# The last MLP of a transformer block: two feature groups by pairs of tiles, and a second product by blocks with seven products of sums

## The chip, the cores and the metric

One core of one Trainium2 chip runs the whole kernel. Its engines work side by side, each through its own queue of instructions: TensorE (PE, products; PEld is its weight load), VectorE (DVE), ScalarE (ACT), GpSimd (POOL) and SyncE (SP, which here only issues transfers). The metric is device microseconds (us) of one launch. An execution taken by the profiler gives the trace; its span is the time from its first to its last instruction.

## The reference, cut to what matters

One block on 1024 tokens of width 1024 in float32: a mixer of two attention kinds, an attention over 256 memory rows, and an MLP with 4096 features, each added to its input. What the change touches is the MLP:

```python
def _sq_relu_mlp(h, w_ff_in, w_ff_out):
    return jnp.square(jax.nn.relu(h @ w_ff_in)) @ w_ff_out
...
        x = x + _sq_relu_mlp(_rms_norm(x, norm3_g[l]), w_ff_in[l], w_ff_out[l])
```

`w_ff_in` is 1024x4096 and `w_ff_out` 4096x1024, both float32.

## The kernel before

**Tiles and split products.** Tokens are handled in 8 tiles of 128 rows. A float32 product is made of three products of a reduced type (float32r): every operand is split into a high part (`hi`, a rounded copy) and a low part (`lo`, the rest), and hi·hi, hi·lo and lo·hi are added in PSUM (`mm`, L218). `split_w` (L244 and L249) does this for weights: ACT copies `hi`, and the subtraction for `lo` is done by POOL or by DVE as the list `PLAN_TAIL` says; in the last part it is ("ag", "av", "ag"), so two of three subtractions are POOL's. A few products (W_out, W_xq, W_xo in the stage `between`) use whole float32 operands instead, one instruction that shows as two records in the trace.

**Order of the work.** A scheduler writes out the order in which each engine's instructions stand, from a model of their lengths; on the chip each engine then takes its queue strictly in that order, and waits where an operand or a buffer is not ready. Buffers are rings (`RINGS`): a tag has a number of buffers, and a new tile waits until the tile that many places before it is done with. The PSUM tags of the main part are S, PT and D with 2 buffers each, and PV and M with 1.

**Stages.** `attend` runs the attention of all tiles; beside it `fill` runs the rest: `between` (output projection, memory attention, L902 on) for tiles 0-1 and 2-3, `mlp` for tiles 0-3, and `between` for tiles 4-5. Behind the attention, `between` for tiles 6-7 is merged with what is left of `fill`. Last comes `mlp(d2, 4, 4, x2s)`, the MLP of tiles 4 to 7, with nothing beside it. Tiles 4 and 5 have been stored to DRAM by then (`x2_dr`) and are read back; tiles 6 and 7 are kept on chip.

**The MLP.** It normalises and transposes the four tiles (`norm_T2`: ACT square L293, POOL power L231, DVE scaling L297, PE transposes L274, copies L235 and L236), then takes the 4096 features in 8 groups of four times 128 (`f4`). In each group: 96 products of 512 columns make the features of all four tiles (4 features x 8 slices of the width x 3); for each feature ACT does relu and square (L1034, L1035) and POOL the split (L1037, L1038). Then 96 products of 512 columns multiply them by a slice of `w_ff_out` (2 column halves x 4 tiles x 4 features x 3), and DVE adds each of the 8 PSUM results to the tile (`add_to`, L899). The weights come in 256 KB loads issued by SP (L254). In the last group each finished half tile is stored (L1057).

Of the kernel before, what the change touches and what calls it, by code (L numbers as in the profile page):

```python
# [9 lines left out]
F32 = mybir.dt.float32  # L10
F32R = mybir.dt.float32r
# [5 lines left out]
AF = mybir.ActivationFunctionType  # L17
ALU = mybir.AluOpType
# [4 lines left out]
P = 128  # L23
L = 1024
DM = 1024
# [7 lines left out]
NCMP = 63  # L33
KG = 2
NS = 4
RINGS = {
    "p1": {"x4": 5, "st": 2, "relu": 4, "wraw": 4, "whi": 6, "wlo": 6, "c8": 4, "c4": 2, "kraw": 5, "pc": 2},
    "p2": {"x4": 3, "st": 1, "relu": 2, "whi": 4, "wlo": 4, "c8": 3, "c4": 1, "kraw": 4, "pc": 2},
    "dn": {"b4": 4, "h": 8, "relu": 2, "wraw": 2, "whi": 4, "wlo": 4},
    "d2": {"b4": 4, "h": 8, "relu": 2, "wraw": 3, "whi": 6, "wlo": 6},  # L40
}
PSUMS = {"p1": {"D": 4, "M": 3, "C": 1}, "main": {"S": 2, "PT": 2, "PV": 1, "D": 2, "M": 1}}
TAGS = {"p1": ("D", "M", "C"), "p2": ("D", "M", "D"), "dn": ("D", "M"), "d2": ("S", "PT")}
PLAN_HEAD = ("ag", "av")
PLAN_MAIN = ("ag",)
PLAN_TAIL = ("ag", "av", "ag")

SLC, WIN, DSA, IDX = 0, 2, 4, 5

# [31 lines left out]
REST = 70.0  # L81


def drain(gen):
    for _ in gen:
        pass
# [19 lines left out]
def merge(a, b):  # L106
    drain(beside(*a, *b))
# [59 lines left out]
def build(nc, tc, I, C, out):  # L167
    v, s, g, te = nc.vector, nc.scalar, nc.gpsimd, nc.tensor
    ctx = ExitStack()
    W = {n: I[n][0] for n in I}  # L170
# [7 lines left out]
    p1 = p1_pool.__enter__()  # L178
    psum.update(pool=p1_psum.__enter__(), n=PSUMS["p1"])

    def pst(tag, shape):
        return psum["pool"].tile(shape, F32, tag=tag, name="ps" + tag, bufs=psum["n"][tag],
                                 padded_shape=[P, 512 // int(np.prod(shape[2:]))] + list(shape[2:]))

    def ring(pool, tag, shape, dt=F32):
        n = RINGS[pool.name if isinstance(pool.name, str) else "dn"][tag]
        return pool.tile(shape, dt, tag=tag, name=tag, bufs=n)

    def row(ap):
        return ap[None, :]  # L190
# [26 lines left out]
    def mm(o, a, b, start, stop):  # L217
        te.matmul(o, a, b, start=start, stop=stop)  # L218
# [21 lines left out]
    def split_w(raw, hi, lo):  # L240
        h, l = plan["w"][plan["i"] % len(plan["w"])]
        plan["i"] += 1
        if h == "a":
            s.activation(hi, raw, AF.Copy)  # L244
        elif h == "v":
            v.tensor_copy(hi, raw)
        else:
            g.tensor_scalar(hi, raw, 1.0, 1.0, op0=ALU.mult, op1=ALU.mult)
        (v if l == "v" else g).tensor_tensor(lo, raw, hi, op=ALU.subtract)  # L249
# [40 lines left out]
    def norm_T2(pool, x_t, gb, xs):  # L290

        ss = small(pool, "nss", 1)
        s.activation(xs[0], x_t.rearrange("p (k c) -> p k c", c=P), AF.Square, accum_out=ss)  # L293
        r = rsqrt_of(pool, ss, DM, 1, "n")
        for c in range(0, DM, 512):
            xn = ring(pool, "relu", [P, 512])
            v.scalar_tensor_tensor(xn, x_t[:, c:c + 512], r[:, 0:1], gb[c // 512], op0=ALU.mult, op1=ALU.mult)  # L297
            to_T(pool, xn, [x[:, c // P:c // P + 4] for x in xs], 4)
# [65 lines left out]
    x2_dr = [dr.tile([P, DM], F32, tag=f"x2{t}", name=f"x2{t}") for t in range(NT)]  # L364
# [534 lines left out]
            v.tensor_tensor(dst, pt, dst, op=ALU.add)  # L899
        return add_to  # L900

    def between(pool, t0, nt, x2s, keep):  # L902

        o_of = []
        for t in range(nt):
# [1 line left out]
            for c in range(8):  # L907
                nc.sync.dma_start(o[:, c, :], oT_dr[t0 + t][c])
            o_of.append(o)
        x2 = [ring(pool, "b4", [P, DM]) for t in range(nt)]  # L910
        for t in range(nt):
            nc.sync.dma_start(x2[t], I["x"][0, (t0 + t) * P:(t0 + t + 1) * P, :])
        add_to = residual_add(x2)
# [2 lines left out]
        _, xf, xt_of = xT(pool, nt, True)  # L916
# [85 lines left out]
    def mlp(pool, t0, nt, x2s):  # L1002
# [13 lines left out]
        for f4 in range(8):  # L1016
# [24 lines left out]
            for c in range(2):  # L1041
# [4 lines left out]
                for t in range(nt):  # L1046
# [11 lines left out]
                                          x2[t][:, c * 512:(c + 1) * 512])  # L1058
                    yield 2.6

    def pe_stack():
        pe = p1.tile([P, 2, 32], F32R, tag="pe", name="pe")
        pe2 = ring(p1, "relu", [P, 2, 2, 64])
        for j in range(2):
            nc.sync.dma_start(pe2[0:32, :, j, :], W["nsa_cmp_pe"].rearrange("k l d -> l k d"))
        pp = pst("M", [P, 2, 32])
        for kv in range(2):
            te.transpose(pp[:, kv, :], pe2[0:32, kv, :, :].rearrange("p a d -> p (a d)"), ident[0:32, 0:32])
        s.activation(pe, pp, AF.Copy)
        v.tensor_tensor(pe[64:128], pp[64:128], pe[64:128], op=ALU.subtract)  # L1070
        return pe
# [45 lines left out]
    rest = fill()  # L1117
    together(attend(aw, st), rest, projected)
    aw_pool.__exit__(None, None, None)
    at_pool.__exit__(None, None, None)  # L1120
    d2_pool = tc.tile_pool(name="d2", bufs=1, side="right", reuse_waits="tile")
    plan["w"] = PLAN_TAIL
    d2 = d2_pool.__enter__()
    x2s = {}
    rest = (w for w in rest if not isinstance(w, tuple))
    merge((rest, REST), (between(d2, 6, 2, x2s, True), 45.0))
    dn_pool.__exit__(None, None, None)
    drain(mlp(d2, 4, 4, x2s))
    d2_pool.__exit__(None, None, None)
    ctx.close()  # L1130


# [19 lines left out]
```

## Time and profile before

| | |
|---|---|
| median of 3 runs | 1837.35 us (1835.46 to 1839.35) |
| time of the profiled execution | 1835.75 us |
| its span, first to last instruction | 1833.9 us |
| mean granted TensorE clock | 0.970 of full speed |
| PE busy, share of the span | 1726.9 us, 94% |
| DVE, ACT, POOL busy | 936.1, 1074.6, 895.0 us |
| last MLP, first product to last | from 1468.8 to 1830.2 us |

Times in the trace are us from the start of the span. Busy time of a matmul includes its passage through the array, which overlaps the next one; the rate of products is read from the distance of their starts. A bracket behind a row names the idle time ahead of the instruction and what ended it. Some matmul records are missing from a trace, so starts are counted over whole patterns (hi·hi, lo·hi, hi·lo repeat in threes).

### The profile page before, as it was taken

The page shows a single profiled execution, that of the slowest core. Times are in us where ns is not written, and L with a number is a line of the kernel's source. Part 1 is how long each engine was busy: PE and PEld are TensorE (multiplying, and loading weights), DVE is VectorE, ACT ScalarE, POOL GpSimd, SP SyncE. Part 2 cuts the span into 40 slices and gives each one's busy share as a digit, 9 for nine tenths or more (in the row PEclk, how much of TensorE's full clock was granted, in tenths as well). Part 3 has the DMA queues.
Part 4 walks back from the last instruction along what each step waited for, and adds up shares of the span by engine and source line. Part 5 has one row for each costly group of instructions (what it writes and reads, how often), then busy time and mean ns, then how long its engine had stood idle before and what let it go on. Part 6 is the DMA issues. An engine that isn't in the chain of part 4 may idle for free. (4 is left out here: it accounts for less than half of the span.)

```text
span 1833.9 us, 28049 instructions
## 1 busy us (share of the span) xinstructions
PE 1726.9 (94%) x9262; PEld 1474.2 (80%) x9262; DVE 936.1 (51%) x2353; ACT 1074.6 (59%) x2687; POOL 895.0 (49%) x1034
## 2 busy tenths in 40 slices
PE   5996999889989998999999999999999799999999
PEld 5995988777878787778887788888988578787787
DVE  4553766575684678466664656646523422222222
ACT  4444658889588669955797457994412323333332
POOL 2364657446262244677676576662111144454443
PEclk9997998999999999999999999999989799999999
DMA  8224512256335320222112112125394222222232
GB/s 203 70 87 160 103 34 79 78 193 180 122 112 162 120 81 24 73 81 71 64 63 91 54 65 75 60 79 185 99 288 131 71 69 92 92 93 93 94 99 98
DMA packets 180081, 187.50 MB, mean 102 GB/s; under 512 B 34656, under 2 KB 149088, under 8 KB 179936
## 3 DMA queue, kind: packets, MB, share of 16 engines
q1 hardware_dynamic: 172000, 175.23, 30.8%
q0 software_dynamic: 7936, 10.49, 2.2%
q8 instruction: 73, 1.20, 0.3%
q14 instruction: 72, 0.59, 0.1%
HBM read 164.69 MB, written 20.97 MB: 101 GB/s over the span
## 5 line engine op out<-in xcount | busy, mean ns | idle before, releaser
L249 POOL TENSOR_TENSOR wlo<-wraw,whi 128x512 fp32r<-128x512 f32 (+1 forms) x230 | 308.5, 1347 | 278.7 <-ACT whi L244 247.6
L244 ACT ACTIVATE whi<-wraw 128x512 fp32r<-128x512 f32 (+2 forms) x289 | 181.1, 628 | 247.4 <-PE psS L218 147.1
L218 PE MATMUL psD<-whi,xh 128*128 128x256 f32 (+1 forms) x704 | 193.8, 359 | 3.6 <-ACT whi L244 2.9
L218 PE MATMUL psD<-wlo,xh 128*128 128x256 f32 (+1 forms) x704 | 194.8, 357 | 0.8 <-DMA wlo<-in_w_in_dram 0.8
L236 DVE TENSOR_TENSOR pl<-psPT,ph 128x512 fp32r<-128x512 f32 (+1 forms) x232 | 142.2, 621 | 78.2 <-ACT ph L235 75.4
L218 PE MATMUL psD<-whi,h 128*128 128x512 f32 x512 | 174.3, 404 | 1.8 <-POOL h L1037 1.0
L688 ACT ACTIVATE S<-S,mn 128x128 f32<-128x128 f32 (+7 forms) x192 | 142.7, 744 | 41.5 <-DVE mn L686 40.3
L218 PE MATMUL psS<-whi,h 128*128 128x512 f32 x512 | 162.1, 392 | 5.1 <-DVE b L899 5.1
L693 POOL TENSOR_SCALAR S<-S,sums,gi 128x640 f32<-128x640 f32 (+7 forms) x128 | 107.7, 850 | 106.7 <-DVE sums L691 99.0
L235 ACT ACTIVATE ph<-psPT 128x512 fp32r<-128x512 f32 (+1 forms) x232 | 122.8, 540 | 60.9 <-PE psPT L703 54.5
L249 DVE TENSOR_TENSOR wlo<-wraw,whi 128x512 fp32r<-128x512 f32 (+1 forms) x59 | 64.3, 1090 | 166.9 <-ACT whi L244 166.8
L218 PEld LDWEIGHTS psD<-whi,xh 128*128 128x128 f32 x704 | 134.0, 198 | 14.3 <-ACT whi L244 3.3
L218 PEld LDWEIGHTS psD<-wlo,xh 128*128 128x128 f32 x704 | 134.8, 197 | 12.5 <-DMA wlo<-in_w_in_dram 1.2
L703 PE MATMUL psPT<-c_ident,S 128*128 128x128 f32 x816 | 132.3, 279 | 8.3 <-DVE ql L236 4.2
L899 DVE TENSOR_TENSOR b<-psS,b 128x512 f32<-128x512 f32 (+1 forms) x80 | 50.0, 635 | 152.6 <-PE psS L218 152.6
L218 PEld LDWEIGHTS psS<-whi,h 128*128 128x128 f32 x512 | 96.1, 188 | 29.3 <-DVE b L899 9.3
L218 PE MATMUL psS<-K,qh 128*128 128x384 f32 (+3 forms) x288 | 113.5, 397 | 5.6 <-DVE mn L686 2.8
L218 PEld LDWEIGHTS psD<-whi,h 128*128 128x128 f32 x512 | 95.6, 190 | 23.7 <-DVE b L899 1.5
L703 PEld LDWEIGHTS psPT<-c_ident,S 128*128 128x128 f32 x816 | 98.1, 143 | 18.9 <-POOL S L693 5.6
L218 PE MATMUL psD<-wlo,h 128*128 128x512 f32 x256 | 102.5, 404 | 1.3 <-POOL wlo L249 1.3
L218 PE MATMUL psD<-xh,wlo 128*128 128x512 f32 x256 | 101.5, 398 | 0.0
L899 DVE TENSOR_TENSOR b<-psD,b 128x512 f32<-128x512 f32 (+1 forms) x112 | 63.2, 572 | 74.5 <-PE psD L218 73.0
(299 smaller groups left out, 4647.4 us busy)
## 6 DMA issues: line engine op xcount, KB each, us to landing
wraw<-in_w_ff_in_dram SPq DMA_DIRECT2D x128, 256.0 KB, 2.7
wraw<-in_w_ff_out_dram SPq DMA_DIRECT2D x128, 256.0 KB, 2.6
whi<-in_w_out_dram SPq DMA_DIRECT2D x32, 256.0 KB, 5.0
wlo<-in_w_out_dram SPq DMA_DIRECT2D x32, 256.0 KB, 4.6
wraw<-in_w_in_dram SPq DMA_DIRECT2D x24, 256.0 KB, 3.1
q<-st SPq DMA_DIRECT2D x12, 512.0 KB, 2.6
qin<-q SPq DMA_DIRECT2D x44, 128.0 KB, 2.3
x<-in_x_dram SPq DMA_DIRECT2D x8, 512.0 KB, 5.2
```

Of the source, the lines that this page charges most:

```text
L218: te.matmul(o, a, b, start=start, stop=stop)
L235: s.activation(hi, src, AF.Copy)
L236: v.tensor_tensor(lo, src, hi, op=ALU.subtract)
L244: s.activation(hi, raw, AF.Copy)
L249: (v if l == "v" else g).tensor_tensor(lo, raw, hi, op=ALU.subtract)
L688: s.activation(S, S, AF.Exp, bias=low, scale=-1.0, accum_out=sums[:, hh:hh + 1])
L693: g.tensor_scalar(Ss[hh], Ss[hh], sums[:, hh:hh + 1], 1.0 if gate is None else gate[:, hh:hh + 1], op0=ALU.mult, op1=ALU.mult)
L703: te.transpose(p2[:, j, hh, :], S[:, (c + j) * P:(c + j + 1) * P], ident)
L899: v.tensor_tensor(dst, pt, dst, op=ALU.add)
```

## The change

`mlp` for tiles 4-7 is replaced by `mlp_tail`. Feature groups 0 and 1 (`G = 2`) are done for tiles 4-5 first (`group(f4, (0, 1), False)`) and for tiles 6-7 at the very end (`group(f4, (2, 3), ...)`), each time with 256 columns in the first product, and with their weights loaded and split once for each pair. The other six groups are done for all four tiles between the two (`group_seven`). Their first product is as before. Their second product is cut into 2x2 blocks, on the side of the features (two halves of the tokens by two halves of the group's features) and on the side of `w_ff_out` (two halves of the features by two halves of the columns), and seven block products of sums and differences take the place of eight (Strassen's method in Winograd's form). Each of the seven is 2 tiles x 2 features x 3 = 12 products of 512 columns, so 84 in place of 96. The sums of features (`rows`, 512 columns) and of weights (`cols`, 1024 columns) are DVE's, four of each for a group; each operand is split after its sum is taken, so there are 14 weight splits in place of 8 and 7 feature splits in place of 4. The seven results are summed over the six groups in `acc` (14 additions for a group; copies by ACT in the first), and `put_together` adds them to the tiles at the end: 7 DVE additions of 1024 columns and 8 of 512.

`PLAN_TAIL` is now ("ag", "av"): every second weight subtraction is DVE's. Weight loads of this part are 512 KB each. Rings of the stages concerned get other sizes, and the pool of the new part (`d3`) lies where the pool of `fill` (`dn`) lay. The order in which the engines' instructions stand is the same as before up to the last part of `between` for tiles 4-7.

```diff
+G = 2
 RINGS = {
...
-    "d2": {"b4": 4, "h": 8, "relu": 2, "wraw": 3, "whi": 6, "wlo": 6},
+    "res": {"b4": 4},
+    "d2": {"b4": 2, "h": 8, "relu": 2, "whi": 4, "wlo": 4},
+    "d3": {"g": 2, "h": 12, "relu": 2, "wraw": 4, "whi": 10, "wlo": 10},
+    "d4": {"r": 2, "hsum": 4, "wsum": 3},
...
-PLAN_TAIL = ("ag", "av", "ag")
+PLAN_TAIL = ("ag", "av")
...
+        def features(f4, ts):
+            cols = slice(ts[0] * P, (ts[-1] + 1) * P)
+            for f2 in range(2):
+                gr = []
+                for k0 in range(0, 8, 4):
+                    c0 = (f4 * 4 + f2 * 2) * P
+                    raw = ring(pool, "wraw", [P, 4, 256])
+                    nc.sync.dma_start(raw, W["w_ff_in"][k0 * P:(k0 + 4) * P, c0:c0 + 256].rearrange("(k p) n -> p k n", p=P))
+                    for k in range(0, 4, 2):
+                        hi, lo = ring(pool, "whi", [P, 2, 256], F32R), ring(pool, "wlo", [P, 2, 256], F32R)
+                        split_w(raw[:, k:k + 2, :], hi, lo)
...
+        def down(pt, hs, ws, us):
+            for f, ((hh, hl), (wh, wl)) in enumerate(zip(hs, ws)):
+                mm(pt, hh[:, us], wh, f == 0, False)
+                mm(pt, hh[:, us], wl, False, False)
+                mm(pt, hl[:, us], wh, False, f == len(hs) - 1)
...
+            def product(i, a, b):
+                hh, hl = ring(pool, "h", [P, 2, 256], F32R), ring(pool, "h", [P, 2, 256], F32R)
+                s.activation(hh, a, AF.Copy)
+                g.tensor_tensor(hl, a, hh, op=ALU.subtract)
+                ws = []
+                for f in range(2):
+                    hi, lo = ring(pool, "whi", [P, 512], F32R), ring(pool, "wlo", [P, 512], F32R)
+                    split_w(b[:, f, :], hi, lo)
+                    ws.append((hi, lo))
+                for t in range(2):
+                    pt = pst(("D", "S", "PT")[(2 * i + t) % 3], [P, 512])
+                    down(pt, [(hh[:, f, :], hl[:, f, :]) for f in range(2)], ws, slice(t * P, (t + 1) * P))
+                    if f4 == G:
+                        s.activation(acc[:, i, t, :], pt, AF.Copy)
+                    else:
+                        v.tensor_tensor(acc[:, i, t, :], pt, acc[:, i, t, :], op=ALU.add)
+
+            product(0, A[0][0], B[0][0])
+            product(1, A[0][1], B[1][0])
+            s1 = rows(A[1][0], A[1][1], ALU.add)
+            t1 = cols(B[0][1], B[0][0])
+            product(4, s1, t1)
+            s2, t2 = rows(s1, A[0][0]), cols(B[1][1], t1)
+            product(5, s2, t2)
+            product(3, A[1][1], cols(t2, B[1][0]))
+            product(2, rows(A[0][1], s2), B[1][1])
+            product(6, rows(A[0][0], A[1][0]), cols(B[1][1], B[0][1]))
...
+        for ts in ((0, 1), (2, 3)):
+            for t in ts:
+                start(t)
+            if ts[0] == 0:
+                for f4 in range(G):
+                    group(f4, ts, False)
+        with tc.tile_pool(name="d4", bufs=1, side="right", reuse_waits="tile") as more:
+            acc = more.tile([P, 7, 2, 512], F32, tag="acc", name="acc")
+            for f4 in range(G, 8):
+                group_seven(more, f4, acc)
+            put_together(acc)
+        for t in (0, 1):
+            nc.sync.dma_start(out[0, (t0 + t) * P:(t0 + t + 1) * P, :], x2[t])
+        for f4 in range(G):
+            group(f4, (2, 3), f4 == G - 1)
...
-    drain(mlp(d2, 4, 4, x2s))
     d2_pool.__exit__(None, None, None)
+    with tc.tile_pool(name="d3", bufs=1, reuse_waits="tile") as d3:
+        mlp_tail(d3, res, x2s, 4)
```

More of the change, by code (lines that the diff above doesn't have):

```diff
@@ L39 @@
     "dn": {"b4": 4, "h": 8, "relu": 2, "wraw": 2, "whi": 4, "wlo": 4},
-    "d2": {"b4": 4, "h": 8, "relu": 2, "wraw": 3, "whi": 6, "wlo": 6},
+    "res": {"b4": 4},
+    "d2": {"b4": 2, "h": 8, "relu": 2, "whi": 4, "wlo": 4},
+    "d3": {"g": 2, "h": 12, "relu": 2, "wraw": 4, "whi": 10, "wlo": 10},
+    "d4": {"r": 2, "hsum": 4, "wsum": 3},
 }
 PSUMS = {"p1": {"D": 4, "M": 3, "C": 1}, "main": {"S": 2, "PT": 2, "PV": 1, "D": 2, "M": 1}}
-TAGS = {"p1": ("D", "M", "C"), "p2": ("D", "M", "D"), "dn": ("D", "M"), "d2": ("S", "PT")}
+TAGS = {"p1": ("D", "M", "C"), "p2": ("D", "M", "D"), "dn": ("D", "M"), "d2": ("S", "PT"), "d3": ("D", "M")}
 PLAN_HEAD = ("ag", "av")
 PLAN_MAIN = ("ag",)
-PLAN_TAIL = ("ag", "av", "ag")
+PLAN_TAIL = ("ag", "av")
 SLC, WIN, DSA, IDX = 0, 2, 4, 5
@@ L900, in residual_add, with between @@
         return add_to
-    def between(pool, t0, nt, x2s, keep):
+    def between(pool, t0, nt, x2s, keep, res=None):
         o_of = []
@@ L909, in between @@
             o_of.append(o)
-        x2 = [ring(pool, "b4", [P, DM]) for t in range(nt)]
+        x2 = [ring(res or pool, "b4", [P, DM]) for t in range(nt)]
         for t in range(nt):
@@ L1120, in build @@
     at_pool.__exit__(None, None, None)
+    res_pool = tc.tile_pool(name="res", bufs=1, side="right", reuse_waits="tile")
+    res = res_pool.__enter__()
     d2_pool = tc.tile_pool(name="d2", bufs=1, side="right", reuse_waits="tile")
@@ L1125, in build @@
     rest = (w for w in rest if not isinstance(w, tuple))
-    merge((rest, REST), (between(d2, 6, 2, x2s, True), 45.0))
+    merge((rest, REST), (between(d2, 6, 2, x2s, True, res), 45.0))
     dn_pool.__exit__(None, None, None)
-    drain(mlp(d2, 4, 4, x2s))
     d2_pool.__exit__(None, None, None)
+    with tc.tile_pool(name="d3", bufs=1, reuse_waits="tile") as d3:
+        mlp_tail(d3, res, x2s, 4)
+    res_pool.__exit__(None, None, None)
     ctx.close()
```

88 lines of the change are left out of this document (added).

## The prediction

> **What bounds the kernel now.** I read the page first (busy shares, slices, last chain), then the chain in order of time for the last MLP, then the engines by windows, then single rows for rates.
>
> ```profile
> PE 1726.9 (94%) x9262; PEld 1474.2 (80%) x9262; DVE 936.1 (51%) x2353; ACT 1074.6 (59%) x2687; POOL 895.0 (49%) x1034
> ...
> PE   5996999889989998999999999999999799999999
> ...
> PE 19%; DVE 1%; issue 0%
> ```
>
> PE is full nearly everywhere; the one 7, the 32nd slice of 45.8 us, lies from 1421 to 1467, just ahead of the last MLP. The chain that ends last is PE with DVE additions between:
>
> ```profile
> 1468.06 1.08 PE psPT L274 x4
> 1469.14 28.00 PE psS L218 x119
> ...
> 1542.80 44.12 PE psS L218 x191
> 1586.92 0.02 issue
> 1586.94 0.70 DVE b L899
> 1587.65 0.04 issue
> ...
> 1830.18 0.69 DVE b L899
> ```
>
> So a feature group takes 44.12 + 0.77 = 44.9 us: PE's products, and one wait for a PSUM buffer that DVE has to empty. The windows show the hole and the dense part:
>
> ```profile
> 1420.50:1468.80 48.30, 36.20 (x154) 28.47 (x152) 19.58 (x45) 16.48 (x34) 7.99 (x9) 0.73 0.22 71
> ...
> 1542.80:1587.70 44.90, 44.34 (x193) 36.02 (x193) 11.11 (x15) 14.59 (x24) 21.14 (x18) 1.00 0.29 94
> ```
>
> Columns: length; busy of PE, PEld, DVE, ACT, POOL with counts; granted clock; DMA share; GB/s. Ahead of the MLP PE idles and its clock is at 0.73. In the MLP only PE is full; DVE, at 11.1 of 44.9 us, has room.
>
> **Rates of PE,** from starts over whole patterns:
>
> ```profile
> 1480.82 0.40 PE L218 MATMUL psS<-xh,wlo 128*128 128x512 f32 x1
> ...
> 1491.26 0.40 PE L218 MATMUL psS<-xh,wlo 128*128 128x512 f32 x1
> ...
> 1498.24 0.39 PE L218 MATMUL psS<-wlo,h 128*128 128x512 f32 x1
> ...
> 1512.55 0.39 PE L218 MATMUL psS<-wlo,h 128*128 128x512 f32 x1
> ```
>
> The first pair is 45 products apart: 10.44/45 = 0.232 us for a product of the first kind. The second is 63 apart: 14.31/63 = 0.227 us. A group's 192 products thus need 96 x 0.232 + 96 x 0.227 = 44.1 us, as the chain says. Products of 256 columns with the same operands stand in the first stage:
>
> ```profile
> 108.63 0.28 PE L218 MATMUL psD<-wlo,xh 128*128 128x256 f32 x1
> ...
> 111.70 0.28 PE L218 MATMUL psD<-wlo,xh 128*128 128x256 f32 x1
> ```
>
> By the pattern of three these are 27 apart: 3.07/27 = 0.114 us, no worse than half of 0.232.
>
> **Term 1, the hole, -21.4 us.** As the changed program stands, the features of tiles 4-5 are queued on PE between the pieces of `between` for tiles 6-7, where PE now idles, and the transposes of tiles 6-7 stand among second products.
>
> ```profile
> 1403.59 0.60 PE L972 MATMUL psPT<-c_ident,relu 128*128 128x128 f32 x4
> 1404.03 1.03 PE L218 MATMUL psD<-whi,xh 128*128 128x256 f32 x4
> ...
> 1405.57 1.64 PE L218 MATMUL psS<-h 128*128 128x128 f32 x12
> 1407.05 1.08 PE L218 MATMUL psD<-whi,xh 128*128 128x256 f32 x4
> ...
> 1436.25 1.09 PE L274 MATMUL psPT<-c_ident,relu 128*128 128x128 f32 x4 [3.01 <-DMA relu<-xo]
> ...
> 1444.32 1.03 PE L218 MATMUL psS<-wlo,xh 128*128 128x256 f32 x4
> ...
> 1454.68 1.03 PE L218 MATMUL psS<-wlo,xh 128*128 128x256 f32 x4
> ...
> 1458.68 1.34 PE L274 MATMUL psPT<-c_ident,relu 128*128 128x128 f32 x8 [2.98 <-DVE relu L297]
> ```
>
> What PE must do from 1420.5 to 1468.8, at full clock: four transposes take 0.44 us, so its 52 take 5.7; 12 small products take 1.48, so 24 take 3.0; 12 of 256 columns take 1.4 at 0.114; the 48 records from 1444.32 to 1454.68 give 0.216 each, so W_xo's 64 take 13.8. Sum 23.9 of 48.3: 24.4 us can be filled, if 87 us of pair work is ready in time. It isn't at once:
>
> ```profile
> 1411.76 0.34 SPq L1000 DMA_DIRECT2D x<-b  x1
> ...
> 1419.84 0.32 SPq L1007 DMA_DIRECT2D b<-x  x1
> 1420.25 2.27 SPq L254 DMA_DIRECT2D wraw<-in_w_ff_in_dram  x2
> ```
>
> Tiles 4-5 are written from 1411.8 on, read back up to 1419.8, and the first weights follow on SP's queue. Normalisation and splits put the first feature at about 1424; I leave 3 us unfilled. That queue is also where xo of tiles 6-7 now stands behind weight loads that wait for ring buffers; those delays fall on `between`, which the pairs cover. POOL's queue keeps the key and value loads of tiles 6-7 ahead of the new splits.
>
> **Term 2, the seven products, -16.3 us.** 12 x 6 = 72 products fewer at 0.227. **Term 3, 256 columns, -0.9 us:** two groups x (192 x 0.114 - 96 x 0.232). **Term 4, old waits, -8.8 us.** From 1468.8, where the hole's window ends with the first product, to the chain's last addition at 1830.2 the MLP takes 361.4 us, its products 8 x 44.1 = 352.6; the rest is the wait above, eight times, and a cold start. All of it is replaced by the new waits of term 5.
>
> **Term 5, new waits, +24 us.** First the load on the others.
>
> ```profile
> L249 DVE TENSOR_TENSOR wlo<-wraw,whi 128x512 fp32r<-128x512 f32 x38 | 43.7, 1150 | 139.9 <-ACT whi L244 139.9
> L899 DVE TENSOR_TENSOR b<-psS,b 128x512 f32<-128x512 f32 x64 | 43.2, 688 | 112.1 <-PE psS L218 112.1
> ...
> L249 POOL TENSOR_TENSOR wlo<-wraw,whi 128x512 fp32r<-128x512 f32 x76 | 101.4, 1342 | 124.7 <-ACT whi L244 123.8
> L1038 POOL TENSOR_TENSOR h<-relu,h 128x512 fp32r<-128x512 f32 x28 | 37.1, 1327 | 1.7
> ...
> L244 ACT ACTIVATE whi<-wraw 128x512 fp32r<-128x512 f32 x108 | 68.3, 632 | 161.5 <-PE psS L218 117.7 <-DMA wraw<-in_w_ff_in_dram 40.2 <-DMA wraw<-in_w_ff_out_dram 0.9
> ...
> 1703.86 1.84 DVE L249 TENSOR_TENSOR wlo<-wraw,whi 128x512 fp32r<-128x512 f32 x1 [7.19 <-ACT whi L244]
> ...
> 1713.60 0.69 DVE L249 TENSOR_TENSOR wlo<-wraw,whi 128x512 fp32r<-128x512 f32 x1 [7.90 <-ACT whi L244]
> ...
> 1703.86 1.29 POOL L1038 TENSOR_TENSOR h<-relu,h 128x512 fp32r<-128x512 f32 x1
> ...
> 1713.66 1.79 POOL L1038 TENSOR_TENSOR h<-relu,h 128x512 fp32r<-128x512 f32 x1
> ```
>
> The last four rows matter most. DVE's subtraction takes 0.69 us when it starts ahead of POOL's, and POOL's then takes 1.79 for 1.29; started together with it, DVE's takes 1.84. An addition with one operand in PSUM takes 0.69 always. So DVE instructions with two operands in SBUF hold up POOL, and POOL them, and all the new sums are of that kind. [...]
>
> A seven-product group of 22.3 + 84 x 0.227 = 41.3 us of PE asks of ACT 22 + 8 + 7 instructions of 0.63 = 23 us; of POOL 11 weight and 7 feature subtractions, 24 us; of DVE 14 additions at 0.69 (9.6), 11 weight subtractions and 4 row sums at 1.15 (17.2), and 4 column sums, with twice the elements, at 2 x 0.69 to 2 x 1.15 (I take 1.9, 7.6): 34.4 us. Nobody passes PE, but the queues are strict. Behind the last feature come relu, square and copy on ACT, three of that 0.63, and POOL's subtraction (1.33), which has one weight subtraction ahead that starts on a slot the last feature frees: about 4 us. PE has the first block product and four matmuls of the next ready, 16 x 0.227 = 3.6. So 0.4 us is the floor; POOL then feeds a part of 1.33 for each product of 2.7, with weight subtractions and DVE's locks between, and three or four such holds at a bad place give 5. I take 2, nearer the floor, since most weight splits and column sums stand in the features' 22 us: 6 x 2 = 12.
>
> Pairs: after a pair's last feature two ACT and two POOL instructions of half size, at most (0.63 + 0.63 + 1.33 + 1.33)/2 = 2.0, against nine products not needing the last feature, 2.0; floor 0.3, with a POOL instruction ahead twice 2.7; I take 1.5, four times 6. Their weights come twice as fast as the 94 GB/s of the window above; bandwidth costs nothing by this row:
>
> ```profile
> 1340.00:1360.00 20.00, 19.33 (x81) 16.36 (x81) 2.35 (x9) 0.70 (x2) 0.62 (x2) 0.91 1.09 347
> ```
>
> The way out of the seven groups: DVE's queue holds 15 fold additions (7 double), 12 to 22 us, and weight splits ahead of the PSUM additions of tiles 6-7; with two PSUM buffers PE then stops after its first two results. Its features (96 x 0.114) and these two results (24 x 0.227) cover 11 + 5 us; floor 2 (a split that waits for a weight slot stands ahead), ceiling 10; I take 5. Another 1 for the way in.
>
> **Sum.** -21.4 - 16.3 - 0.9 - 8.8 + 24 = -23.4; 1835.75 - 23.4 = 1812.3 for an execution like the profiled one, which lies 1.6 under the median of 1837.35, so 1814.
>
> **Rivals.** *DVE becomes the bound (slower).* If every two-operand DVE instruction first waits out a POOL instruction of 1.34, DVE needs 9.6 + 15 x 2.03 + 4 x 2.7 = 51 us a group, 7.7 over my 43.3: 1814 + 46 = 1860. It decides from 47 us a group, a mean wait of 1.1 us; the mean seen is 1.15 - 0.69 = 0.46. Chance 0.08. [...] Chance 0.15. *The hole stays,* because the reload of tiles 4-5 or buffers shared with the earlier pool come late: term 1 falls, 1835. For it: SP's strict queue; against it: 48 us to be late in. Chance 0.05. *The scheduler's order hides nearly all waits,* 8 of the 24 us left: 1798. Chance 0.13.
>
> **Numbers.** My forecast keeps 0.59, 1806 to 1822 by its own bounds (seven-groups 1 to 3 us). The range 1798 to 1834 leaves out the first rival, most of the third and a little below. A measurement of this kernel tells about 0.2%, 3.7 us, from no change: faster 0.87, same 0.05 (the third rival), slower 0.08.
>
> **What would show it.** Right: no slice under 9 near the old hole and a clock near 1.0 there; a seven-product group of 43 to 44 us in the chain; DVE near 80% there, its column sums near 1.9 us; one larger PE wait for DVE after the sixth group. Wrong: chain rows of DVE or POOL that carry more than a tenth of a seven-product group, features of tiles 4-5 that start after 1435, or a clock under 0.9 in the pairs.

## The result and the profile after

The changed kernel takes 1830.15 us (median; 1824.91 to 1833.16) where the kernel before, run beside it, takes 1837.35 (1835.46 to 1839.35): a ratio of 0.9954, 95% interval 0.9934 to 0.9974. That is 7 to 8 us gained; 23 were forecast. A later set of runs of the same two kernels gave 0.9951 (0.9936 to 0.9967). The profiled execution is its fastest: 1824.91 us, span 1823.1.

On the page, the row of PE and its slices and the slices of the granted clock:

```profile
PE 1700.3 (93%) x9382; PEld 1457.0 (80%) x9382; DVE 1088.6 (60%) x2493; ACT 1144.6 (63%) x2827; POOL 965.0 (53%) x1057
...
PE   5996999889989998999999999999999889999987
...
PEclk9998999999999999999999999999989899999998
```

PE is busy 26.6 us less than before (1726.9), DVE 152 us more. The one 7 of the old hole is gone, but two 8s stand in its place (slices 32 and 33, 1413 to 1504 us: the start of the old hole, and the way into the seven-product groups), and an 8 and a 7 end the row, where the kernel before had 9s. The stages that follow are counted from one row that stands in every trace, the transposes of the first of the two queries in the second half of the memory attention of tiles 6-7 ("the landmark" below; before, then after):

```profile
1420.52 0.38 PE L274 MATMUL psPT<-c_ident,relu 128*128 128x128 f32 x2
...
1411.73 0.38 PE L278 MATMUL psPT<-c_ident,relu 128*128 128x128 f32 x2
```

The same by windows: from the landmark to the first feature of the seven-product groups, then the six groups, then the last pairs; below them two single groups.

```profile
1411.70:1499.60 87.90, 76.69 (x438) 67.85 (x436) 47.57 (x76) 43.31 (x88) 42.69 (x42) 0.88 0.53 167
1499.60:1759.00 259.40, 251.19 (x1078) 200.38 (x1079) 177.73 (x182) 136.99 (x235) 165.29 (x107) 1.00 0.30 93
1759.00:1823.10 64.10, 49.67 (x294) 42.36 (x294) 38.83 (x39) 20.78 (x41) 34.92 (x29) 0.92 0.38 127
...
1629.50:1672.50 43.00, 41.87 (x181) 33.55 (x181) 29.41 (x33) 21.93 (x38) 28.02 (x19) 1.00 0.31 98
1672.50:1715.50 43.00, 41.90 (x181) 33.56 (x181) 31.23 (x33) 22.06 (x38) 28.10 (x19) 1.00 0.33 99
```

(Columns: length; busy of PE, PEld, DVE, ACT, POOL with counts; granted clock; DMA share; GB/s.) The middle runs at full clock (1.00), 42.8 to 43.0 us for each of its second to fifth groups. The two other stages are where clock (0.88 and 0.92) and time are lost. The terms of the prediction, sorted by these stages, set the question:

| us | forecast | how | measured |
|---|---|---|---|
| landmark to first four-tile feature | 74.6 | 48.3 - 21.4 + pairs 43.7 + waits 3 + way in 1 | 87.9 |
| six groups | 259.8 | 6 x 43.3 | 259.4 |
| last pairs to the end | 55.5 | pairs 43.7 + waits 3 + way out 5 + end 3.8 | 64.1 |
| sum (before: 413.4) | 389.9 | | 411.4 |

(A pair group is 96 x 0.114 + 48 x 0.227 = 21.8, two are 43.7; 3.8 is the rest of the span before behind the start of its last addition.) From the landmark on only 2.0 of 23.5 us came. The second profile of the changed kernel repeats the three stages within 0.7 us (87.2, 259.4, 64.1), so differences of several microseconds between stages can be read from single profiles. The other 8.8 us of this execution lie ahead of the landmark and are taken up at the end of the experiments.

The first and the last stage more finely, by windows. The sum of the first four is the first stage:

```profile
1411.70:1425.90 14.20, 7.67 (x33) 5.77 (x31) 11.53 (x25) 8.38 (x21) 6.18 (x6) 0.67 1.01 339
1425.90:1430.30 4.40, 4.35 (x20) 4.35 (x21) 3.32 (x6) 4.14 (x10) 1.45 (x2) 0.50 0.54 153
1430.30:1485.70 55.40, 55.40 (x354) 50.42 (x352) 22.60 (x33) 26.55 (x51) 31.20 (x32) 1.00 0.46 141
1485.70:1499.60 13.90, 9.28 (x34) 7.30 (x33) 10.11 (x14) 4.24 (x7) 3.85 (x4) 0.75 0.30 98
...
1782.00:1788.80 6.80, 0.24 (x1) 0.00 (x0) 6.80 (x9) 1.15 (x2) 2.55 (x2) 0.50 0.53 185
1788.80:1793.00 4.20, 4.11 (x12) 3.26 (x13) 0.63 (x2) 0.00 (x0) 0.00 (x0) 0.61 1.00 325
```

Between 1430 and 1486 PE is full at full clock (55.40 of 55.40 us, 1.00): the pairs do fill what they can, and their own waits are zero. Before that, and on the way into the groups, PE waits and then works at half clock (0.50 from 1425.9 to 1430.3, 0.51 from 1489.7 to 1495.2). By the rates of the prediction the first stage holds 67.6 us of PE work (23.9 and the pairs' 43.7), so 20.3 of its 87.9 us are lost: 12.7 at the start (18.6 us that hold 5.9 us of work) and 7.6 on the way in (13.9 us that hold 6.3). On the way out it stands for 6.8 us, and its clock is at 0.61 for the next 4.2. PE's waits from 1400 us on, by what ended them (total, times, longest):

```profile
PE psD L222 <- DVE b L1135: 7.2, 2, 6.7
PE psM L278 <- DVE xl L240: 3.8, 1, 3.8
PE psPT L222 <- POOL h L1168: 3.4, 6, 0.6
PE psD L222 <- POOL h L1118: 2.4, 2, 2.1
```

The two long ones are the way out (DVE's addition to tiles 6-7) and the way in (the low half of a transposed piece, which frees the one buffer M). The last row is of the way out too: PE waits there for POOL's halves of the features. The seven-product groups have many waits of at most 0.6 us. The chain of waits through one of them and at the end:

```profile
1672.49 22.25 PE psD L222 x97
1694.77 0.69 DVE acc L1180
...
1699.82 3.41 DVE hsum L1156 x2
1703.23 0.61 DVE acc L1180
1703.88 0.73 PE psPT L222 x2
...
1715.49 22.25 PE psD L222 x97
...
1785.75 2.48 DVE wlo L253 x4
1788.23 0.61 DVE b L1135
1788.89 23.81 PE psD L222 x143
```

DVE carries the chain for 9.1 us of a group (1694.77 to 1703.84), but PE is busy for 8.0 of them, and for 41.9 of the group's 43.0.

### The profile page after: what moved, and what is told of

Read it like the earlier page. It is cut to its first block, busy times and chain, and to the rows that moved or that the text cites. A ratio compares the mean times of both kernels' runs of the same rounds, so it can differ in the third digit from the quotient of the medians.

```text
span 1823.1 us, 28548 instructions
## 1 busy us (share of the span) xinstructions
PE 1700.3 (93%) x9382; PEld 1457.0 (80%) x9382; DVE 1088.6 (60%) x2493; ACT 1144.6 (63%) x2827; POOL 965.0 (53%) x1057
## 4 chain that ended last, share of the span: by engine, by line
PE 64%; DVE 13%; POOL 7%; ACT 6%; DMA 5%; issue 5%; SPq 0%; POOLq 0%; DVEq 0%; ACTq 0%
PE psD L222 41%; PE psS L222 10%; PE psPV L222 4%; PE psPT L707 4%; POOL wlo L253 2%; ACT dmask L648 2%; DVE hsum L1156 1%; PE psM L278 1%; DVE wlo L253 1%; POOL S L697 1%; DVE S L690 1%; DMA wraw<-in_w_ff_in_dram 1%; PE psPT L222 1%; DVE pl L240 1%; DVE acc L1180 1%
## 5 line engine op out<-in xcount | busy, mean ns | idle before, releaser
L248 ACT ACTIVATE whi<-wraw 128x512 fp32r<-128x512 f32 (+2 forms) x309 | 192.3, 627 | 148.9 <-PE psD L222 40.8
L222 PE MATMUL psD<-whi,h 128*128 128x512 f32 x760 | 263.7, 407 | 14.3 <-DVE b L1135 7.2
L222 PE MATMUL psD<-xh,wlo 128*128 128x512 f32 (+1 forms) x576 | 213.2, 371 | 0.0
L222 PE MATMUL psD<-xh,whi 128*128 128x512 f32 (+1 forms) x576 | 211.4, 371 | 1.4 <-ACT xh L239 0.8
L222 PE MATMUL psD<-xl,whi 128*128 128x512 f32 (+1 forms) x576 | 212.3, 371 | 0.0
L222 PEld LDWEIGHTS psD<-whi,h 128*128 128x128 f32 x760 | 143.6, 191 | 51.2 <-DVE b L1135 8.2
L222 PE MATMUL psD<-wlo,h 128*128 128x512 f32 x380 | 152.3, 403 | 1.3 <-POOL wlo L253 1.3
L222 PEld LDWEIGHTS psD<-xh,whi 128*128 128x128 f32 x576 | 108.8, 189 | 20.5 <-ACT xh L239 1.6
L222 PEld LDWEIGHTS psD<-xh,wlo 128*128 128x128 f32 x576 | 109.0, 189 | 17.2 <-POOL wlo L253 0.3
L222 PEld LDWEIGHTS psD<-xl,whi 128*128 128x128 f32 x576 | 108.8, 189 | 16.4
```

## The experiments

All times are medians; each ratio is against the kernel before, run on the same chip (1836.3 to 1838.6 us). A stage is given as in the windows above.

### Which half pays

**Pairs alone.** In `mlp_tail` the six middle groups become `group(f4, (0, 1, 2, 3), False)`; the sums, `acc` and `put_together` go.

```
...
-            for f4 in range(G, 8):
-                group_seven(more, f4, acc)
-            put_together(acc)
+        for f4 in range(G, 8):
+            group(f4, (0, 1, 2, 3), False)
```

> The six middle groups do all eight products (their second product as in the pairs, all four tiles), so no sums, no fold; the two pair groups stay. Theory T (the pairs fill the hole but lose 12.7, 7.5 and 15 us at its start, on the way in and on the way out; the seven products bring what was forecast): six groups of 44.9 for 43.0 us cost 11.4, and the way out loses its fold with the 6.7 us wait and the half clock behind it, about 9: about 1832, that is 2 over the changed kernel's 1830. Rival R (the seven products do not pay: the sums and the way out cost more than 72 products): 1822 or less. Rival Q (the pairs brought nothing, all of the gain is the seven products): 1838 or more.

Measured 1822.53 us, ratio 0.9923 (0.9909 to 0.9937): 14 us faster than before, and faster than the changed kernel. By windows (the same three stages):

```profile
1416.30:1503.30 87.00, 75.29 (x437) 66.65 (x435) 46.76 (x74) 43.38 (x88) 42.64 (x42) 0.90 0.55 169
1503.30:1772.00 268.70, 265.31 (x1157) 216.31 (x1157) 67.24 (x97) 87.31 (x144) 116.80 (x96) 1.00 0.33 98
1772.00:1823.20 51.20, 45.24 (x289) 40.30 (x287) 18.46 (x21) 20.00 (x40) 29.09 (x29) 1.00 0.37 114
```

Rival R holds, half a microsecond above its price: in this kernel the seven products cost more than they bring. But they bring 9.3 us in their own stage (268.7 to 259.4), somewhat less than the 11.4 of the theory; 12.9 us are given back in the last one (51.2 to 64.1; 1.4 of them are six products of the sixth group that stand there). Nor is all of the gain of the pairs a filled hole: behind the landmark this kernel is 6.4 us shorter than the kernel before (407.0 for 413.4), and its profile reaches the landmark 4.3 us sooner.

**Seven products alone** (`G = 0`, all four tiles written at the end).

> No pair groups: all eight groups do seven products for four tiles, the hole stays, and the fold ends the program. Theory T: eight groups of 43.0 for 44.9 are 15 us less than the kernel before; the fold, of which about 8 us lie behind the last product, and the write of the result behind it give 11 back: 1833. Rival R (a seven-product group is worth nothing beside the eight): 1846 or more.

Measured 1836.31 us, ratio 0.9994 (0.9981 to 1.0006): no difference from the kernel before, and nearer to theory T than to its rival. The eight groups, with the fold (the additions of `put_together`) and the write bare at the end, take 363.7 us where the eight of the kernel before take 365.2.

### The way out

**No fold.** The call of `put_together(acc)` is taken out.

> The changed kernel without the putting together of the seven sums (its 15 additions are left out, so the output lacks what the six groups add). Theory F (the fold holds up the DVE queue, in which the weight splits of the last pairs stand, and that costs about 12 us on the way out): 1819. Rival L (the way out is slow because the last pairs' weights are loaded and split late, with or without the fold): 1826 or more.

Measured 1812.69 us, ratio 0.9886 (0.9870 to 0.9902). Against the changed kernel's 0.9954 that is 0.0068 of 1837, 12 us; by medians it is 17. The stages:

```profile
1413.50:1501.20 87.70, 76.78 (x438) 68.04 (x436) 47.50 (x76) 43.45 (x88) 43.07 (x42) 0.88 0.54 171
1501.20:1757.20 256.00, 250.15 (x1078) 200.88 (x1079) 171.54 (x183) 137.44 (x235) 166.32 (x107) 1.00 0.31 95
1757.20:1810.30 53.10, 47.15 (x295) 41.28 (x294) 17.69 (x24) 19.95 (x41) 31.21 (x30) 1.00 0.43 137
```

Without the fold the last stage is 11.0 us shorter and the six groups 3.4. Of these 3.4, 3.2 are the sixth group's (40.3 us for 43.5), inside which the fold's first additions stand; the second to fifth take 43.0 us at most in both kernels. So the fold costs 12 to 17 us, and it costs them from the sixth group on. Theory F holds.

**Six PSUM buffers** for the second product of the pairs, the first pairs as well as the last:

```
-                    pt = pst(TAGS[pool.name][0], [P, 512])
+                    pt = pst(("D", "S", "PT")[(2 * c + t) % 3], [P, 512])
```

> The second product of the pair groups goes round six PSUM buffers for two. Theory T: PE no longer stops 6.7 us after two results of the last pairs, nor runs 4 us at half clock behind that stop: 7 to 9 us less than the changed kernel, 1822. Rival W (PE would stop there anyway, for the weight splits that stand in the same DVE queue behind the fold): 0 to 2 us less, 1829.

Measured 1830.24 us, ratio 0.9967 (0.9956 to 0.9978): nothing gained in all, the number of rival W. Of PE's waits behind the sixth group, the one for DVE's addition is gone and a shorter one stands in its place, for the weight splits that the rival named:

```profile
PE psS L222 <- DVE wlo L253: 5.5, 2, 3.8
...
1767.00:1826.30 59.30, 49.77 (x294) 43.74 (x294) 39.38 (x39) 20.46 (x41) 34.87 (x29) 0.93 0.42 137
```

The last stage did get shorter, from 64.1 to 59.3 us. What hides it is the same edit in the first pairs: the first stage grows from 87.9 to 91.2 us, with PE's wait for the low halves on the way in at 10.7 us for 3.8, and the six groups from 259.4 to 261.9.

**Splits off DVE.** `plan["w"] = ("ag",)` ahead of `put_together(acc)`: the last pairs' weight splits go to ScalarE and GpSimd.

> The changed kernel, but the weight splits of the last two pair groups all go to ScalarE and GpSimd, so that behind the seven-product groups DVE holds only the fold and the additions. Theory F (DVE's queue is what is late on the way out): 1822 to 1826. Rival P (GpSimd is then late instead): 1829 or more.

Measured 1835.29 us, ratio 0.9984 (0.9968 to 1.0000): 5 us slower than the changed kernel, as rival P had it. The last stage by windows, with POOL (fifth engine) now busy 51.7 of 69.7 us:

```profile
1761.40:1831.10 69.70, 51.38 (x294) 43.99 (x294) 26.86 (x24) 20.61 (x40) 51.74 (x45) 0.88 0.36 114
```

**Half the splits** of the last pairs (`if k == 0 or len(ts) == 4 or ts[0] != 2:` ahead of the split in `features`, and the same with `i` in `group`; the other pieces use the halves of the piece before, so their products are of wrong weights).

> The changed kernel, but the pairs of tiles 6-7 at the end split only every second piece of their weights (left out as in the other kernel). The fold stays as it is. Theory D (on the way out PE waits for splits that share their queue with the fold): 8 to 12 us less than 1830, 1818 to 1822. Rival A (PE waits for the fold's additions ahead of its own results): 1827 or more.

Measured 1825.57 us, ratio 0.9934 (0.9918 to 0.9950): 4 to 5 us less than the changed kernel, half of what theory D expected and more than its rival. The last stage takes 61.8 us. **Both edits together:**

> The changed kernel with both edits on the way out: the second product of the pairs goes round six PSUM buffers, and the pairs of tiles 6-7 split only every second piece of their weights (the others' splits are left out). Theory B (PE waits behind the fold for splits and for PSUM buffers in turn, so that either alone hides the other): 1815 to 1820, near the 1813 of the kernel without the fold. Rival T (a third thing is late there, the loads or GpSimd): 1824 to 1826, as with half the splits alone.

Measured 1827.29 us, ratio 0.9939 (0.9921 to 0.9957): by the time, no more than the splits alone, as rival T said. By the stages it is nearer to theory B:

```profile
1767.50:1823.20 55.70, 47.44 (x294) 41.57 (x294) 29.49 (x31) 13.55 (x28) 24.13 (x22) 1.00 0.44 147
```

The last stage, 64.1 us in the changed kernel, is 59.3 with six buffers, 61.8 with half the splits, 55.7 with both, and 53.1 with no fold. So the two edits together take away 8.4 of the fold's 11.0 us there, more than the sum of each alone. The time does not show it because the six buffers lengthen the first stage, here to 93.3 us (87.7 with half the splits alone). Which of the splits' engines matters this does not say, since ACT, POOL and DVE all lose work and weight buffers come free sooner. For the 2.6 us that are left, the rows of POOL and DVE in the changed kernel name a candidate. POOL's view, first in the first pairs, then beside the fold:

```profile
1477.58 0.75 POOL L1119 TENSOR_TENSOR h<-relu,h 128x256 fp32r<-128x256 f32 x1
1478.30 0.41 POOL L1118 TENSOR_SCALAR h<-relu 128x256 fp32r<-128x256 f32 x1
...
1766.02 3.97 POOL L253 TENSOR_TENSOR wlo<-wraw,whi 128x512 fp32r<-128x512 f32 x2
1769.97 1.37 POOL L1118 TENSOR_SCALAR h<-relu 128x256 fp32r<-128x256 f32 x1
1771.42 1.59 POOL L1119 TENSOR_TENSOR h<-relu,h 128x256 fp32r<-128x256 f32 x1
```

and DVE's at the same time:

```profile
1749.10 2.32 DVE L1200 TENSOR_TENSOR acc<-acc 128x1024 f32<-128x1024 f32 x1
...
1766.53 2.31 DVE L1203 TENSOR_TENSOR acc<-acc 128x1024 f32<-128x1024 f32 x1
...
1776.48 1.77 DVE L253 TENSOR_TENSOR wlo<-wraw,whi 128x512 fp32r<-128x512 f32 x1
1778.18 7.65 DVE L1199 TENSOR_TENSOR b<-b,acc 128x512 f32<-128x512 f32 x6
1785.75 2.48 DVE L253 TENSOR_TENSOR wlo<-wraw,whi 128x512 fp32r<-128x512 f32 x4
1788.16 1.28 DVE L1135 TENSOR_TENSOR b<-psD,b 128x512 f32<-128x512 f32 x2
```

The fold's 15 additions sum to 23.1 us in this profile. They stand in DVE's queue ahead of most of the splits and of the additions of the last pairs, and while they run, POOL's halves of the features take up to 1.37 and 1.59 us for 0.41 and 0.75, and its weight splits 2 us for 1.3. So the pairs' DVE work waits, and POOL's is slowed: PE waits 3.3 us for POOL's halves on the way out, and 1.0 in the kernel without the fold. The queue of the loads waits too: from 1720 to 1800 SP's DMA issues wait for DVE's splits to free their buffers,

```profile
SPq L1127 <- DVE wlo L253: 27.8, 8, 13.2
```

where the kernel without the fold shows 11.1 us for this line's waits on DVE. What POOL and the loads cost by themselves was not tried.

**The fold beside PE work.** Five groups with seven products, then one of eight for all four tiles, the fold written behind it:

```
-            for f4 in range(G, 8):
+            for f4 in range(G, 7):
                 group_seven(more, f4, acc)
+            group(7, (0, 1, 2, 3), False)
             put_together(acc)
```

> Five groups with seven products; the last group of the four tiles does eight, and the fold is written behind it, so that its 22 us of features and 22 us of products lie beside the fold. Theory F: one group more at 44.8 for 43.2 us costs 1.6, the way out loses 3 for 12 to 15 us: 1821 to 1823. Rival L: 1829 or more. Rival S (the seven-product groups themselves cost more in most executions than in the profiled one): 1827.

Measured 1817.38 us, ratio 0.9902 (0.9888 to 0.9915), some 4 us better than theory F and 5 us under the pairs alone, with intervals that still overlap a little. The last two stages:

```profile
1504.10:1765.60 261.50, 254.35 (x1097) 204.30 (x1098) 176.63 (x181) 130.54 (x223) 163.62 (x106) 1.00 0.33 101
1765.60:1816.80 51.20, 45.22 (x289) 40.27 (x287) 20.18 (x22) 20.00 (x40) 29.24 (x29) 0.99 0.37 113
```

The last stage is the 51.2 us of the kernel with no fold in it, and the middle is 7.2 us under that of eight products throughout. Seven products pay once 44 us of PE work with few DVE instructions lie beside the fold.

### The first stage

**Sums of tiles 4-5 kept in SBUF.** `between(dn, 4, 2, x45, True)`, and two `s.activation(x2s[t], x45[t], AF.Copy)` into the pool `res`.

> The sums of tiles 4-5 stay in SBUF: ScalarE copies them (two copies) to the buffers of the last MLP, where the changed kernel writes them to DRAM and reads them back. Theory T (the start of the hole is lost to the chain write 4.27, read 6.02, then norm, which loads the DMA too): the first feature of tiles 4-5 starts 6 to 9 us sooner, and the time is 5 to 7 us less, 1824. Rival V (the DVE queue, where norm stands between the steps of the other tiles, sets that start): the first feature starts under 3 us sooner and the time is within 2 us of 1830.

Measured 1830.00 us, ratio 0.9963 (0.9950 to 0.9977). Rival V: the first feature of tiles 4-5 starts 13.5 us behind the landmark for 14.2, so the round trip through DRAM hides.

**Transposes through two buffers** (`"d3": ("D", "PT")`, in the kernel with pairs alone).

> The kernel with the pairs and eight products throughout (1822.5), with the transposes of tiles 4-7 ahead of the last MLP in the two PSUM buffers PT for the one buffer M. Theory B (on the way in PE waits 4 us for DVE because there is one buffer, and runs at half clock behind it): 1817 to 1819. Rival D (the transposes wait for their input from DVE, whichever buffer they have): 1821 to 1823.

Measured 1831.38 us, ratio 0.9978 (0.9964 to 0.9991), 9 us worse than the kernel that it alters; neither theory had that. The buffers PT also serve the transposes of tiles 6-7, and the order on PE changes: the first feature of tiles 4-5 starts 36.7 us behind the landmark for 14.8, and the first stage grows from 87.0 to 94.7 us, with PE waiting 6.1 us for a load of xo. So this is no test of the one buffer M by itself.

**Four buffers in the ring relu,** with the fold beside the eight-product group, and in the changed kernel (`"relu": 4`):

> The version with the fold beside an eight-product group (1817.4), with four buffers for two in the ring relu of the last MLP, which the normed pieces of tiles 6-7 share with the features of the pairs. Theory N (the norm of tiles 6-7 waits for GpSimd to free these buffers, and that makes the way in 7.5 us longer): 1812 to 1814. Rival D (DVE's queue and the one buffer M set the way in): 1816 to 1818.

> The changed kernel with the four relu buffers and nothing else. Theory N: 1825 to 1827. Rival D: 1829 to 1831.

Measured 1815.58 us, ratio 0.9888 (0.9869 to 0.9907), and 1828.37, ratio 0.9948 (0.9936 to 0.9961). Against the kernels without it that is 0.0014 and 0.0006, inside the intervals; nearer to rival D, and PE's wait of 3.8 us on the way in is still there. **With the sums kept as well:**

> The version with the fold beside an eight-product group and four relu buffers, with the sums of tiles 4-5 kept in SBUF. Keeping them alone brought nothing. Theory K (the order that it brought gave back what the start of the hole gained, since tiles 6-7 wait for relu buffers): 3 us less than without it, 1809 to 1811. Rival V (DVE's queue sets the start of the hole): the same as without it within 2 us.

Measured 1820.44 us, ratio 0.9901 (0.9887 to 0.9915): by the ratio 2 us more than without it, by the median 5. Theory K falls.

**One pair group** (`G = 1`, fold beside an eight-product group).

> The version with the fold beside an eight-product group (1817.4), with one feature group by pairs for two: six groups with seven products, one with eight. Theory H (the hole is 48 us and lacks 24 us of work, one pair group of 22 us nearly fills it, and the pairs' losses lie at its start whatever their number): 2.1 less for the sixth seven-product group, and up to 6 less for a way in with no pair work left over: 1809 to 1815. Rival G (with less pair work PE waits for tiles 6-7 instead): 1818 or more.

Measured 1819.78 us, ratio 0.9906 (0.9888 to 0.9924): the same as with two, and the number of rival G. The first stage with no pairs (the kernel of seven products alone) and with one pair group:

```profile
1418.40:1471.40 53.00, 35.34 (x150) 28.52 (x148) 27.77 (x54) 18.50 (x40) 10.67 (x10) 0.70 0.41 134
```

```profile
1416.30:1482.30 66.00, 51.70 (x295) 44.38 (x292) 36.83 (x66) 31.09 (x64) 27.48 (x26) 0.87 0.56 172
```

With two it is 85.6 (fold beside the eight-product group). So the first pair group of 21.8 us of work makes the stage 13.0 us longer and the second 19.6. PE's own work is 23.9, 45.7 and 67.6 us: 29, 20 and 18 us are lost. So the hole takes in 9 us of the first pair group and 2 of the second, and never its 24. It is the latency of a chain of small steps, and the chain moves: the last W_xo products of tiles 6-7 start 41 us behind the landmark with no pair group, 54 with one and 55 with two. The first group moves the chain's end; the second lies nearly all behind it.

**Half the splits** of the first pairs (as above with `ts[0] != 0`, in the kernel with four relu buffers).

> The version with the fold beside an eight-product group and four relu buffers (1815.6), but the pairs of tiles 4-5 split only every second piece of their weights and use its halves for the next piece as well (left out: the other pieces' splits, so the products of these two groups are of the wrong weights). PE's work and the loads are unchanged. Theory D (the splits of the pairs, at twice the rate of a four-tile group, share DVE's and GpSimd's queues with the steps of tiles 6-7 and the norms, and that sets the start of the hole and the way in): 6 to 9 us less, 1807 to 1810. Rival C (the chain of loads and of the other tiles' own steps sets them): 0 to 2 us less, 1814 to 1816.

Measured 1811.42 us, ratio 0.9857 (0.9836 to 0.9879), 4 us under the kernel that it alters. The first stage of that kernel, and of this one:

```profile
1413.40:1498.70 85.30, 74.22 (x438) 65.24 (x436) 48.92 (x76) 42.78 (x88) 43.45 (x42) 0.92 0.56 170
```

```profile
1414.90:1493.90 79.00, 71.85 (x437) 63.55 (x435) 39.31 (x66) 33.74 (x70) 29.73 (x33) 0.96 0.57 188
```

6.3 us of the stage go with half of the splits: theory D by the stage, a little less by the median. The first feature of tiles 4-5 starts 2.0 us sooner (11.5 us behind the landmark for 13.5), and PE's wait for the low halves on the way in falls from 4.0 to 1.5 us. Some 11 of 79 us stay lost.

### Ahead of the landmark

> The kernel before, unchanged, for a second profile. Theory J (what lies ahead of the changed part differs by chance from execution to execution, by the granted clock): the landmark, 1420.5 in the first profile, comes at 1412 to 1419, like those of the kernels with the change. Theory E (the change speeds up the pieces ahead of it as well): at 1419 to 1423 again.

> The changed kernel unchanged, beside the other: 1830, and a second profile of it.

The kernel before: 1837.75 us, ratio to the same kernel 1.0001 (0.9982 to 1.0020), landmark at 1421.7. The changed kernel: 1829.38, ratio 0.9951 (0.9936 to 0.9967), landmark at 1412.7, and 410.7 us from there to the end. So theory E: 1420.5 and 1421.7 before; 1411.7, 1412.7 and, in 13 other kernels with the change 1413.4 to 1418.5 (in the two that keep the sums, transposes of tiles 4-5 come ahead of this row). Some 4 us of it come in the last 90 us ahead of the landmark: from the 217th of DVE's reductions and reciprocals (1331.4 us in the first profile of before) to the landmark it is 89.1 and 91.1 us before, and 84.8 to 87.1 with the change. The end of that stretch by windows of the first profile of before, and of after (equal clock times, not exactly the same instructions):

```profile
1335.00:1421.00 86.00, 83.91 (x434) 74.14 (x432) 26.47 (x75) 17.68 (x43) 10.11 (x18) 0.95 0.68 213
```

```profile
1335.00:1411.00 76.00, 76.00 (x403) 67.63 (x403) 24.51 (x69) 15.61 (x40) 6.78 (x11) 0.98 0.59 188
```

PE has no idle left there and a higher granted clock after the change (0.98 for 0.95); the order of its instructions differs from about 1340 us on. What in the change orders them so was not tried. The rest of the difference at the landmark lies where the instructions stand in the same order and varies from execution to execution. From the landmark on the change is worth 2 to 3 us (413.4 and 413.6 before, 411.4 and 410.7 after), and ahead of it 2 to 10 by the rows above; the 7 to 8 us of the medians lie in that.

## Why the prediction was right or wrong

**Right:** the direction, PE as the bound, and the price of the seven products. Term 2 with its part of term 5 said 43.3 us a group; 43.0 came, with the fold or without it. The column sums were to take 1.9 us and took 1.23 to 1.76 in the group from 1672.5, the row sums 1.17 to 1.78 for 1.15; DVE was to be near 80% and was at 68 to 73%. The one larger PE wait for DVE after the sixth group is there too. The waits of the pairs (6 in all) were too high in the middle of the first stage: none. Of the signs of being wrong, two came: the clock is under 0.9 in the stage of the first pairs (0.88), and DVE rows carry a fifth of a group's chain, twice the tenth that was asked. The second misled, since PE had other products ready meanwhile.

**Wrong, the way out of the seven groups (term 5): 5 us, ceiling 10; the fold costs 12 to 17.** The step saw the fold's length (12 to 22 us; 23.1 measured) and took the PSUM additions of tiles 6-7 as what waits behind it, with 16 us of PE work as cover. That was half of it: six buffers for those additions shorten the last stage by 4.8 of the 11.0 us that the fold costs there. But the cover itself needs splits, and behind six buffers PE waits for those; half of them left out as well takes another 3.6: a pair group consumes weights at twice the rate of a four-tile group, so in the same 23 us DVE was already due for half of the pairs' splits, and POOL, which had the other half, was slowed by the fold (two splits in 3.97 us, where one behind the fold takes 1.30). The prediction noted the double rate and checked it only against DMA bandwidth.

**Wrong, term 1, the hole:** 24.4 us fillable less 3. With the way in, the first stage came out 13.3 us over: 20.3 us were lost where the sum had 7, that is 12.7 at the start for 3, 7.6 on the way in for 1, and none in the pairs for 3. (The 87 us of pair work set against the hole are those of all four tiles; the 43.7 of tiles 4-5 are all that can lie there. They would have been enough.) The first feature was to come at about 1424 on the clock of the profile before, 3.5 us behind the landmark; it came 14.2 behind it. The step counted PE's work against PE's idle time. But the hole's end is the end of the chain of tiles 6-7, and the pair work lengthens it: it stands ahead of them on PE, and its splits stand between their steps on DVE and POOL. The last W_xo products of tiles 6-7 start 34 us behind the landmark before, 41 with seven products alone, where no pairs stand ahead of them, and 56 after:

```profile
1468.06 1.03 PE L222 MATMUL psS<-wlo,xh 128*128 128x256 f32 x4
```

The norm and the transposes follow only then, with 17 us of pair work left to cover them (PE's next wait begins at 1485.7). Halving the pairs' splits gave 6.3 us back (85.3 to 79.0, where 74.6 were forecast); the rest of the cause stays open, beyond its being neither the DRAM round trip nor the relu ring.

**Missing:** that PE paid twice for its stops here, by the idle time and by the clock behind it. The granted clock is 0.50 for the 4.4 us behind the start of the hole, 0.51 for 5.5 us (1489.7 to 1495.2) behind the stop of 3.8 us on the way in, and 0.61 for the 4.2 us behind the stop of 6.8 us. How long a stop has to be for that, no run shows: at the start of the hole the clock fell though no stop was over 2.0 us, and on the way out it is at 0.50 from the start of the long stop (1782.0 to 1788.8). Also missing, on the other side: the gain ahead of the landmark.

**The rivals.** DVE did not become the bound of a group, and a group lost no more than forecast (2 us a group were taken, 1.7 came: 43.0 less 41.3 of PE work). No run shows the locks that term 5 counts in these 2 us by themselves; what the kernel before shows is two holds, in the prediction's rows: 1.79 us for 1.29 on POOL and 1.84 for 0.69 on DVE. The order did not hide nearly all waits. The hole did not stay in its place, but nearly in its size: 24.4 us lost before, 20.3 in the first stage after; of the two reasons that this rival gave, the reload was none (keeping the sums brought nothing) and shared buffers were not tried. That two-operand DVE work holds up POOL was right and in the wrong place: it is seen most beside the fold (1.59 us for 0.75). What the list of rivals lacked was the one that happened: the seven products lose at their end what they gain in the middle, so that the pairs alone, at 0.9923, beat both together.

**The version that beats both:** five seven-product groups, one of eight with the fold behind it, four relu buffers: 1815.58 us, 0.9888 (0.9869 to 0.9907).

## What to carry to other kernels

When an algorithm saves products in a loop and pays with a fold at its end, price the fold by what the same engine owes to the work that is to cover it, not by that work's PE time; put it beside a part that needs little of that engine. An idle stretch of the bounding engine that comes from a chain of small dependent steps is not a reservoir: work put into it stands in the chain's queues and moves its end. Read an experiment by stages too: an edit that helps one stage and hurts another looks like nothing in the time. Test the two halves of a two-part change apart before believing their sum.

## What the runs showed of the hardware

A one-input GpSimd instruction is held up as well: in the changed kernel 128x256 goes from 0.41 us to 0.84 and 1.37 beside DVE's back-to-back instructions with two operands in SBUF, and the subtraction of the same size from 0.75 to 1.59. Single executions of one kernel lie up to 12 us apart (1831.81 to 1843.74 for the kernel before, in one set of runs), and a part of such differences arises in code that is the same: the 217th of DVE's reductions and reciprocals starts at 1331.4 us in the first profile of the kernel before and at 1325.4 in that of the changed kernel. That is why a difference of a few microseconds between two kernels was taken from medians, and from profiles only by stages behind the landmark.
